# Two-layer hybrid decoder trunk on one Trainium2 core: up products of pairs 2 to 16 joined into 512-column matmuls, the first weight chunk split between two engines, a quarter of the last update on ScalarE and GpSimd

## The chip, the cores and the metric

The kernel runs on one core of one Trainium2 chip. The metric is device time in microseconds (us), lower is better: the median of several executions. The engines are PE (TensorE, the matrix engine, which takes its weights by separate load instructions, PEld), DVE (VectorE), ACT (ScalarE), POOL (GpSimd) and SP (SyncE, which here only issues DMAs). They run side by side and meet at semaphores.

## The reference, cut to what matters

Two layers over 256 positions of 1024 features, fp32. Each layer is an attention half (two attention mixers that are gated and merged) and a gated feed-forward half. The change touches the feed-forward half, the first projection and the last residual update.

```python
def rms_norm(x, gain): ...                    # x * rsqrt(mean(x*x) + EPS) * gain
def conv_ffn(h, w_up, conv_w, conv_b, w_down):
    u = h @ w_up                              # 1024 -> 2 * 2816
    up = jnp.pad(u, ((0, 0), (CONV_WIDTH - 1, 0), (0, 0)))
    c = conv_b
    for k in range(CONV_WIDTH):               # causal, depthwise, width 3
        c = c + conv_w[k] * up[:, k:k + s]
    a, val = jnp.split(c, 2, axis=-1)
    return (jax.nn.gelu(a, approximate=True) * val) @ w_down

def hybrid_layer(x, ...):
    h = rms_norm(x, attn_pre_gain)
    u = h @ w_in                              # the first projection
    ...
    x = x + rms_norm(mixed @ w_out, attn_post_gain)
    h = rms_norm(x, ffn_pre_gain)
    return x + rms_norm(conv_ffn(h, ...), ffn_post_gain)
```

## The kernel before, in words

**Numbers.** Every operand of a matmul is split into a high and a low part (type fp32r): the high part is a rounded copy, the low part what is left. A product is then three matmuls into one PSUM bank: high by high, high by low, low by high. So a tile of weights that arrives as `st` becomes `wh` (a copy on ACT, L114) and `wl` (a subtraction on DVE, L117). These two helper lines carry most of the work of ACT and DVE.

**The weight stream.** The object `W` brings all weights in order: a DMA on SP's queue (L160) into `st` (4 buffers), then the copy and the subtraction into `wh` and `wl` (4 buffers each). A buffer of `wh` is free when PE has used the tile four places earlier in the stream, so ACT's copies follow PE. Some tiles are made ahead of their place into buffers that are idle by then ("early" tiles, with the names kB, sg, kA/vbd and q): in the first layer one at each of the pairs 14 to 17 of the feed-forward loop, in the second only at 14 and 16.

**The feed-forward half** (`ffn_layer`). The 5632 columns of the up projection are 22 pairs j = 0 to 21 of a gate half and a value half, 128 columns each. Pairs 0 and 1 come from `up_first` with another tiling. For j = 2 to 20 a loop runs, in this order on PE:

- `up(j, half)`, twice: for each of 8 blocks k of the features three matmuls 128x256 (L1065 to L1067), moving the tile hh (high), hl (low) and hh again, 24 in all; both halves lie in one bank, T or mm in turn;
- `down(j-2)`: 12 matmuls 128x512 (L388 to L390 in the helper `mm3`) into four banks (named S and O) that gather the result over all j.

`act_gate(j)` stands between them on the other engines: per half a scaled copy of the bank with bias (ACT, L1048) and two multiply-adds shifted by one and two positions (DVE, L1051 and L1052; together the convolution), then the gelu (ACT, L1072), the product of the halves (DVE, L1073), and its split into gh (ACT, L114) and gl (DVE, L117). These small tiles, all named k, come from one pool of 11 buffers.

**The order.** A scheduler sets each engine's order of instructions from the program; on an engine everything runs in that order.

**The start.** The input x is transposed on PE (L432), multiplied by the first gain on DVE (L434) and split by ACT (L114) and DVE (L117) into the tiles named x. The first weight chunk has 2 blocks of 512 columns and is split as a whole (ACT, 128x1024, then DVE). The first 12 products (L457, each 128x512) use it for both halves t of the positions; next on PE are the transposes of the second chunk of x.

**The end.** `post_norm(t)` adds the normed result to X: ACT takes squares (L407), DVE multiplies by the gain (L408), POOL makes the reciprocal root (L376, L377), and DVE does two updates of 128x512 (L413), each followed by its output DMA (L1169).

Of the kernel before, what the change touches and what calls it, by code (L numbers as in the profile page):

```python
# [16 lines left out]
P = 128  # L17
T = 256
# [35 lines left out]
WARM = (6, 2, 3)  # L54
FIRST = [(0, 0), (1, 0), (0, 1), (1, 1), (0, 2), (1, 2), (0, 3), (1, 3)]
# [10 lines left out]
def tile_hybrid_trunk(  # L66
# [78 lines left out]
    class Stream:  # L145
# [31 lines left out]
        def high(self, i):  # L177
# [20 lines left out]
            copy(hi, st)  # L198

            def low():  # L200
                sub(lo, st, r32(hi))
# [12 lines left out]
    TAGS = {"kB": 1, "sg": 2, "q8": 3}  # L214
# [228 lines left out]
    def attn_layer(l, xp, rs, gains, first, order, last_T):  # L443
# [6 lines left out]
        def products(t, c, bk, chs, w):  # L450
            todo = [(tt, p, k) for p in ((0, 0), (0, 1), (1, 0)) for tt in range(2) for k in range(2)] if c == 0 else \
                   [(t, p, k) for p in ((0, 0), (1, 0), (0, 1)) for k in range(2)]
            if c == 0:
                todo = todo[6 * t:6 * t + 6]
# [108 lines left out]
        qA, qB, qR = big8("q8", 3), big8("q8", 3), big8("q8", 3)  # L563
# [148 lines left out]
        def out_T(br, g):  # L712
            if OT[br] is None:
                OT[br] = big8("q8", 3)
# [247 lines left out]
        return yp  # L962

    def out_layer(l, yp, gains, order):
# [34 lines left out]
        hp = big8("q8", 3), big8("q8", 3)  # L999
# [28 lines left out]
        return hp, [lambda: t4_of(xg[1], hp, 1, 0), lambda: (t4_of(xg[1], hp, 1, 1), low())]  # L1028


    def ffn_layer(l, hp, gains, last, order, last_T):
        hh, hl = hp
# [12 lines left out]
        def conv(b, jj, half, then=None):  # L1045
            c = k1()
            u = b[:, half * T:(half + 1) * T]
# [7 lines left out]
        up_bank, up_w, gs, wdn = {}, {}, {}, {}  # L1055

# [12 lines left out]
        def act_gate(j):  # L1069
            b = up_bank.pop(j)  # L1070
            ca, cv = conv(b, j, 0), conv(b, 22 + j, 1)
# [76 lines left out]
        ca = conv(up_bank.pop(j), j, 0)  # L1148
# [4 lines left out]
        cv = conv(up_bank.pop(j), 22 + j, 1, None if last else lambda: lows.append(W.high(nxt[2])))  # L1153
# [57 lines left out]
    def start():  # L1211
# [13 lines left out]
        lw0 = W.high(0)  # L1225
        low0 = first_split(0, 0, m0, xp)
        warm(WARM[1])
        low1 = first_split(1, 0, first_T(1, 0), xp)
        warm(WARM[2])
        lw0()  # L1230
        low0()
# [26 lines left out]
    for l in range(DEPTH):  # L1258

        yp = attn_layer(l, xp, rs, gains, l == 0, order, last_T)  # L1260
        hp, last_T = out_layer(l, yp, gains, order)
# [80 lines left out]
```

## Time and profile before

| what | us |
|---|---|
| device time, median of 3 (lowest, highest) | 775.21 (775.03, 776.46) |
| device time of the profiled execution | 774.85 |
| its span | 772.8 |
| PE busy | 756.8 (98%) |
| DVE busy | 611.1 (79%) |
| ACT busy | 497.9 (64%) |

The profile is of one execution. Its span runs from the first to the last recorded work; 2.05 us of the device time lie around it. A matmul's recorded duration holds the passage through the array, so matmuls that follow each other overlap in the records: what one costs is the distance from its start to the start of the next, and that is read from the timeline.

### The profile page before, as it was taken

To read this page: it belongs to the slowest core of one execution; us is meant where nothing else is said; L and a number is where in the kernel's file an instruction comes from. 1 tells how busy PE (TensorE), PEld (TensorE's weight loads), DVE (VectorE), ACT (ScalarE), POOL (GpSimd) and SP (SyncE) were. 2 spreads that over 40 slices of the span, in tenths; PEclk is the share of its full clock that TensorE was granted. 3 is DMA by queue.
4 is the path that set the end of the run, shared out by engine and by line. 5 is a ranking of instruction groups with operands and counts; after the bars stand their busy time and mean duration, and the time that the engine had idled before them with its cause. 6 is when DMAs were issued, how large, how long until landed. Compare 5 with 4: busy or idle time off the path is not lost.

```text
span 772.8 us, 12863 instructions
## 1 busy us (share of the span) xinstructions
PE 756.8 (98%) x4742; PEld 677.0 (88%) x4742; DVE 611.1 (79%) x1181; ACT 497.9 (64%) x951; POOL 26.9 (3%) x52
## 2 busy tenths in 40 slices
PE   8999999999999999999999999999999999999995
PEld 6888898888899999999878889988888999999994
DVE  7998898687687777777787989985967877777774
ACT  6686986755665555665566979776565655566552
POOL 3000001000000000000010000010010000000000
PEclk9999999999999999999999999999999999999998
DMA  8633265355655556766335224644655656566621
GB/s 333 198 107 122 63 205 190 137 179 178 195 202 182 187 189 191 230 221 209 132 131 157 89 79 136 210 149 148 206 189 163 185 184 191 185 192 219 196 82 55
DMA packets 42345, 131.25 MB, mean 170 GB/s; under 512 B 5375, under 2 KB 5931, under 8 KB 42283
## 3 DMA queue, kind: packets, MB, share of 16 engines
q1 hardware_dynamic: 41707, 129.39, 51.6%
q10 hardware_dynamic: 576, 1.05, 0.4%
q8 instruction: 37, 0.61, 0.3%
q14 instruction: 25, 0.20, 0.1%
HBM read 129.37 MB, written 1.05 MB: 169 GB/s over the span
## 4 chain that ended last, share of the span: by engine, by line
PE 86%; ACT 8%; DVE 3%; issue 1%; DMA 1%; POOL 0%; SPq 0%; DVEq 0%; POOLq 0%; ACTq 0%
PE mm L388 6%; PE mm L389 6%; PE mm L390 6%; PE S L388 5%; PE S L390 5%; PE S L389 5%; PE mm L1067 5%; PE mm L1066 5%; PE mm L1065 5%; PE T L1066 5%; PE T L1065 5%; PE T L1067 5%; PE O L389 4%; PE O L388 4%; PE O L390 4%; ACT k L649 2%
## 5 line engine op out<-in xcount | busy, mean ns | idle before, releaser
L117 DVE TENSOR_TENSOR wl<-st,wh 128x1024 fp32r<-128x1024 f32 (+2 forms) x214 | 253.2, 1184 | 89.4 <-ACT wh L114 86.8
L114 ACT ACTIVATE wh<-st 128x1024 fp32r<-128x1024 f32 (+2 forms) x214 | 219.1, 1027 | 158.1 <-PE mm L1066 36.8
L1065 PE MATMUL mm<-q,wh 128*128 128x256 f32 x336 | 95.1, 283 | 0.0
L1067 PE MATMUL mm<-q,wl 128*128 128x256 f32 x336 | 95.0, 283 | 0.0
L1066 PE MATMUL mm<-q,wh 128*128 128x256 f32 x336 | 95.0, 283 | 0.0
L388 PE MATMUL mm<-wh,x 128*128 128x512 f32 (+2 forms) x240 | 89.8, 374 | 0.1
L389 PE MATMUL mm<-wl,x 128*128 128x512 f32 (+2 forms) x240 | 88.2, 368 | 0.0
L390 PE MATMUL mm<-wh,x 128*128 128x512 f32 (+2 forms) x240 | 88.0, 367 | 0.0
L1066 PE MATMUL T<-q,wh 128*128 128x256 f32 x304 | 86.0, 283 | 0.0
L1067 PE MATMUL T<-q,wl 128*128 128x256 f32 x304 | 86.0, 283 | 0.0
L1065 PE MATMUL T<-q,wh 128*128 128x256 f32 x304 | 85.9, 283 | 0.0
L1065 PEld LDWEIGHTS mm<-q,wh 128*128 128x128 f32 x336 | 64.4, 192 | 0.9
L1066 PEld LDWEIGHTS mm<-q,wh 128*128 128x128 f32 x336 | 64.4, 192 | 0.8
L1067 PEld LDWEIGHTS mm<-q,wl 128*128 128x128 f32 x336 | 64.4, 192 | 0.1
L1065 PEld LDWEIGHTS T<-q,wh 128*128 128x128 f32 x304 | 58.3, 192 | 0.8
L1066 PEld LDWEIGHTS T<-q,wh 128*128 128x128 f32 x304 | 58.3, 192 | 0.7
L1067 PEld LDWEIGHTS T<-q,wl 128*128 128x128 f32 x304 | 58.3, 192 | 0.0
L390 PEld LDWEIGHTS mm<-wh,x 128*128 128x128 f32 x240 | 45.1, 188 | 5.7 <-DVE x L117 0.4
L388 PEld LDWEIGHTS mm<-wh,x 128*128 128x128 f32 x240 | 45.2, 188 | 4.8 <-ACT k L114 0.4
L389 PEld LDWEIGHTS mm<-wl,x 128*128 128x128 f32 x240 | 45.2, 188 | 4.5
L649 ACT ACTIVATE k<-k,mn 128x128 f32<-128x128 f32 (+1 forms) x96 | 42.4, 445 | 7.1 <-DVE mn L646 7.0
L114 ACT ACTIVATE k<-k 128x256 fp32r<-128x256 f32 x72 | 29.1, 413 | 13.0 <-DVE k L1073 6.1
(336 smaller groups left out, 1665.4 us busy)
## 6 DMA issues: line engine op xcount, KB each, us to landing
st<-in_ffn_w_up_dram SPq DMA_DIRECT2D x88, 512.0 KB, 4.0
st<-in_ffn_w_down_dram SPq DMA_DIRECT2D x44, 512.0 KB, 3.6
st<-in_w_in_dram SPq DMA_DIRECT2D x42, 512.0 KB, 3.8
st<-in_w_out_dram SPq DMA_DIRECT2D x16, 512.0 KB, 3.6
st<-in_w_in_dram SPq DMA_DIRECT2D x16, 384.0 KB, 3.2
st<-in_cmp_w_dram SPq DMA_DIRECT2D x16, 256.0 KB, 2.7
st<-in_w_branch_a_dram SPq DMA_DIRECT2D x8, 512.0 KB, 3.5
st<-in_w_branch_b_dram SPq DMA_DIRECT2D x8, 512.0 KB, 3.5
```

What stands on the lines that cost most here:

```text
L114: return act.activation(dst, src, AF.Copy, scale=scale)
L117: return dve.tensor_tensor(dst, a, b, ALU.subtract)
L388: pe.matmul(o, xh, wh, start=first, stop=False, skip_group_check=True)
L389: pe.matmul(o, xh, wl, start=False, stop=False, skip_group_check=True)
L390: pe.matmul(o, xl, wh, start=False, stop=last, skip_group_check=True)
L649: last_exp[0] = act.activation(self.pt[:, hh, s, :], sm[:, :nk], AF.Exp, bias=self.mn[:, i:i + 1], scale=-1.0, accum_out=self.dn[:, i:i + 1])
L1065: pe.matmul(o, wh[:, k, :], hh[:, k, c0:c1], start=(k == 0), stop=False, skip_group_check=True)
L1066: pe.matmul(o, wh[:, k, :], hl[:, k, c0:c1], start=False, stop=False, skip_group_check=True)
L1067: pe.matmul(o, wl[:, k, :], hh[:, k, c0:c1], start=False, stop=(k == 7), skip_group_check=True)
```

## The change

Three edits, one in each of three places.

1. **Pairs 2 to 16 (JOINT).** The high and low parts of the normed input lie side by side in one tile H. `up_joint` runs per block k one matmul of `wh` that moves both parts (512 columns: high by high in the first half of a bank, high by low in the second) and one of `wl` (256 columns, onto the first half). Each half of a pair has a whole bank. `left` then brings the two halves of the bank together: ACT copies the second half to SBUF, DVE adds the first. The convolution reads that sum from SBUF. The three tiles of tag q8 that held these parts and others become H and one q8 tile. Pairs 17 to 21 stay as they were.
2. **The start.** The copy of the first weight chunk is split in two: block 0 on ACT, block 1 on DVE; the copy of x for t = 0 goes ahead of it on ACT; the subtraction too is in two halves; the 12 products come in another order, with those that need x's low part ahead of some that need `wl`.
3. **The last update (t = 1).** Its last 256 of 1024 columns are scaled on ACT and added to X on POOL; DVE does one update of 512 and one of 256 columns. `post_norm` is used here alone.

```diff
+JOINT = range(2, 17)
...
-        def high(self, i):
+        def high(self, i, halves_by=()):
...
-            copy(hi, st)
+            if halves_by:
+                for k, f in enumerate(halves_by):
+                    f(lambda e, k=k: (copy if e is act else dve.tensor_copy)(hi[:, k], st[:, k]))
+            else:
+                copy(hi, st)
...
+                if halves_by:
+                    for k in range(a):
+                        sub(lo[:, k], st[:, k], r32(hi[:, k]))
+                else:
+                    sub(lo, st, r32(hi))
...
     def post_norm(t, banks, gain, follow):
         g, r = norm_a(banks, gain)
+        if t == 1:
+            z = k1()
+            xs = X[:, t, 3 * T:4 * T]
+            act.activation(z, g[1][:, T:2 * T], AF.Identity, bias=0.0, scale=r)
+            pool.tensor_tensor(xs, z, xs, ALU.add)
         for n in range(2):
-            norm_b(t, n, g, r)
+            if t == 1 and n == 1:
+                xs = X[:, t, 2 * T:3 * T]
+                dve.scalar_tensor_tensor(xs, g[1][:, 0:T], r, xs, ALU.mult, ALU.add)
+            else:
+                norm_b(t, n, g, r)
             follow(n)
...
+                todo = [todo[i] for i in (0, 1, 2, 3, 4, 5, 8, 10, 9, 11, 6, 7)][6 * t:6 * t + 6]
...
-        qA, qB, qR = big8("q8", 3), big8("q8", 3), big8("q8", 3)
+        H = ap_.tile([P, 2, KD, T], F32R, tag="h16", name=nm("H"))
+        qA, qB, qR = H[:, 0], H[:, 1], big8("q8", 1)
...
-        def conv(b, jj, half, then=None):
+        def conv(u, jj, then=None):
             c = k1()
-            u = b[:, half * T:(half + 1) * T]
...
+        def up_joint(j, half):
+            b = up_bank[j, half] = bank("mm" if j % 2 == 0 else "T")
+            wh, wl, _ = W.next(8, P)
+            both = b.rearrange("p (s t) -> p s t", s=2)
+            for k in range(8):
+                pe.matmul(both, wh[:, k, :], H[:, :, k, :], start=(k == 0), stop=False, skip_group_check=True)
+                pe.matmul(b[:, 0:T], wl[:, k, :], hh[:, k, :], start=False, stop=(k == 7), skip_group_check=True)
+
+        def left(j, half):
+            if j not in JOINT:
+                return up_bank[j][:, half * T:(half + 1) * T]
+            b = up_bank.pop((j, half))
+            u = k1()
+            copy(u, b[:, T:2 * T])
+            dve.tensor_tensor(u, b[:, 0:T], u, ALU.add)
+            return u
...
-            ca, cv = conv(b, j, 0), conv(b, 22 + j, 1)
+            ua, uv = left(j, 0), left(j, 1)
+            ca, cv = conv(ua, j), conv(uv, 22 + j)
...
-                part(lambda: up(j, half, 0, T))
+                part(lambda: up_joint(j, half) if j in JOINT else up(j, half, 0, T))
...
-        lw0 = W.high(0)
         low0 = first_split(0, 0, m0, xp)
+        by = []
+        lw0 = W.high(0, [by.append, by.append])
+        by[0](act)
...
+        by[1](dve)
         warm(WARM[2])
+        low0()
         lw0()
-        low0()
         low1()
```

**How the order moves.** Numbers behind a name tell one tile from another. First PE, in one half of a pair of the loop, before:

```order
L1065 MATMUL mm_2648<-q_585_2293,wh_2584 128x256
L1066 MATMUL mm_2648<-q_586_2294,wh_2584 128x256
L1067 MATMUL mm_2648<-q_585_2293,wl_2585 128x256
L1065 MATMUL mm_2648<-q_585_2293,wh_2584 128x256
L1066 MATMUL mm_2648<-q_586_2294,wh_2584 128x256
L1067 MATMUL mm_2648<-q_585_2293,wl_2585 128x256
```

and after, the same two blocks of a half and the end of the `down` ahead of them:

```order
L399 MATMUL O_2629<-wh_2639,k_635_2539 128x512
L1084 MATMUL mm_2720<-H_127,wh_2662 128x512
L1085 MATMUL mm_2720<-H_127,wl_2663 128x256
L1084 MATMUL mm_2720<-H_127,wh_2662 128x512
L1085 MATMUL mm_2720<-H_127,wl_2663 128x256
```

Three matmuls of 256 columns have become one of 512 and one of 256, and the two sizes alternate.

Second ACT, through one pair. Before (wh_2930, wh_2960 and wh_3004 are the copies of weights for tiles that PE takes later; T_2834 is the pair's bank):

```order
L114 ACTIVATE wh_2930<-st_2928 128x1024
L1048 ACTIVATE k_697_2895<-T_2834,vec 128x256
L114 ACTIVATE wh_2960<-st_2958 128x1024
L1048 ACTIVATE k_698_2899<-T_2834,vec 128x256
L1072 ACTIVATE k_697_2895<-k_697_2895 128x256
L114 ACTIVATE wh_3004<-st_3002 128x1024
L114 ACTIVATE k_699_2905<-k_697_2895 128x256
```

After (the pair's banks are mm_2720 and mm_2743; the three buffers of weights that follow come free when PE has ended `up(j+1, 0)`, `up(j+1, 1)` and `down(j-1)`):

```order
L115 ACTIVATE wh_2872<-st_2870 128x1024
L115 ACTIVATE k_685_2766<-mm_2720 128x256
L115 ACTIVATE k_686_2769<-mm_2743 128x256
L115 ACTIVATE wh_2891<-st_2889 128x1024
L1069 ACTIVATE k_687_2772<-k_685_2766,vec 128x256
L1069 ACTIVATE k_688_2776<-k_686_2769,vec 128x256
L115 ACTIVATE wh_2914<-st_2912 128x1024
L1111 ACTIVATE k_687_2772<-k_687_2772 128x256
L115 ACTIVATE k_689_2782<-k_687_2772 128x256
```

Two copies out of PSUM are new, and the pair's steps now stand behind other weight copies: before, the first convolution step stood behind the copy into the buffer that the pair's own `up(j, 1)` has just left free; now it stands behind the copy that waits for `up(j+1, 1)`.

DVE in the same place, before:

```order
L117 TENSOR_TENSOR wl_2931<-st_2928,wh_2930 128x1024
L1051 SCALAR_TENSOR_TENSOR k_697_2895<-T_2834,vec,k_697_2895 128x255
L1052 SCALAR_TENSOR_TENSOR k_697_2895<-T_2834,vec,k_697_2895 128x254
L117 TENSOR_TENSOR wl_2961<-st_2958,wh_2960 128x1024
L1051 SCALAR_TENSOR_TENSOR k_698_2899<-T_2834,vec,k_698_2899 128x255
L1052 SCALAR_TENSOR_TENSOR k_698_2899<-T_2834,vec,k_698_2899 128x254
L1073 TENSOR_TENSOR k_697_2895<-k_697_2895,k_698_2899 128x256
L117 TENSOR_TENSOR wl_3005<-st_3002,wh_3004 128x1024
L117 TENSOR_TENSOR k_700_2906<-k_697_2895,k_699_2905 128x256
```

and after:

```order
L118 TENSOR_TENSOR wl_2873<-st_2870,wh_2872 128x1024
L1093 TENSOR_TENSOR k_685_2766<-mm_2720,k_685_2766 128x256
L1093 TENSOR_TENSOR k_686_2769<-mm_2743,k_686_2769 128x256
L118 TENSOR_TENSOR wl_2892<-st_2889,wh_2891 128x1024
L1072 SCALAR_TENSOR_TENSOR k_687_2772<-k_685_2766,vec,k_687_2772 128x255
L1072 SCALAR_TENSOR_TENSOR k_688_2776<-k_686_2769,vec,k_688_2776 128x255
L1073 SCALAR_TENSOR_TENSOR k_687_2772<-k_685_2766,vec,k_687_2772 128x254
L1073 SCALAR_TENSOR_TENSOR k_688_2776<-k_686_2769,vec,k_688_2776 128x254
L118 TENSOR_TENSOR wl_2915<-st_2912,wh_2914 128x1024
L1112 TENSOR_TENSOR k_687_2772<-k_687_2772,k_688_2776 128x256
L118 TENSOR_TENSOR k_690_2783<-k_687_2772,k_689_2782 128x256
```

Two additions are new, and the product and gl now stand one right behind the other.

Third DVE at the start, before (wl_156 is the first weight chunk's low part, the two results L434 are the scaled x of both t):

```order
L434 TENSOR_TENSOR k_68_153<-T_148,gfirst_120 128x512
L434 TENSOR_TENSOR k_72_166<-T_161,gfirst_120 128x512
L117 TENSOR_TENSOR wl_156<-st_83,wh_155 128x1024
L117 TENSOR_TENSOR x_12_119<-k_68_153,x_11_118 128x4x128
L117 TENSOR_TENSOR x_12_119<-k_72_166,x_11_118 128x4x128
```

and after:

```order
L453 TENSOR_TENSOR k_67_152<-T_147,gfirst_120 128x512
L453 TENSOR_TENSOR k_71_165<-T_160,gfirst_120 128x512
L201 CAST wh_155<-st_83 128x512
L118 TENSOR_TENSOR x_12_119<-k_67_152,x_11_118 128x4x128
L118 TENSOR_TENSOR wl_156<-st_83,wh_155 128x512 x2
L118 TENSOR_TENSOR x_12_119<-k_71_165,x_11_118 128x4x128
```

The cast is new on DVE, and the low part of x for t = 0 now stands ahead of that of the weights.

## Rows read from the trace of the kernel before

**Rows 1.** The page's first part (busy time, share of the span and instructions of each engine) and the first line of the chain of waits that ended last, by engine.

```profile
PE 756.8 (98%) x4742; PEld 677.0 (88%) x4742; DVE 611.1 (79%) x1181; ACT 497.9 (64%) x951; POOL 26.9 (3%) x52
...
PE 86%; ACT 8%; DVE 3%; issue 1%; DMA 1%; POOL 0%; SPq 0%; DVEq 0%; POOLq 0%; ACTq 0%
```

**Rows 2.** Busy time by windows of the span. Columns: window, its length, then busy us and instructions of PE, PEld, DVE, ACT and POOL, the granted PE clock, DMA share and GB/s. The first two lie inside the feed-forward loops of the two layers, the third near the start.

```profile
220.00:360.00 140.00, 140.00 (x989) 131.59 (x989) 108.34 (x160) 84.75 (x123) 0.00 (x0) 1.00 0.63 201
...
590.00:750.00 160.00, 160.00 (x1135) 150.55 (x1134) 121.08 (x179) 93.63 (x139) 0.00 (x0) 1.00 0.59 186
...
20.00:30.00 10.00, 10.00 (x47) 8.00 (x46) 10.00 (x16) 6.67 (x9) 0.00 (x0) 1.00 0.88 295
```

**Rows 3.** Timeline of PE where the `up` of one pair ends and its `down` begins (241.04), and the start of the next `down`. Columns: start, duration, engine, line, operation.

```profile
240.80 0.28 PE L1066 MATMUL T<-q,wh 128*128 128x256 f32 x1
240.92 0.28 PE L1067 MATMUL T<-q,wl 128*128 128x256 f32 x1
241.04 0.39 PE L388 MATMUL S<-wh,k 128*128 128x512 f32 x1
241.27 0.39 PE L389 MATMUL S<-wl,k 128*128 128x512 f32 x1
...
243.58 0.39 PE L390 MATMUL O<-wh,k 128*128 128x512 f32 x1
...
249.56 0.39 PE L388 MATMUL S<-wh,k 128*128 128x512 f32 x1
```

**Rows 4.** Timeline of PE in two other places: the first and last of 24 matmuls of 512 columns without a gap, and a change from 512 to 256 columns.

```profile
14.56 0.39 PE L388 MATMUL mm<-wh,x 128*128 128x512 f32 x1
...
19.78 0.39 PE L390 MATMUL mm<-wh,x 128*128 128x512 f32 x1
...
118.98 0.39 PE L390 MATMUL mm<-wh,x 128*128 128x512 f32 x1
119.20 0.28 PE L708 MATMUL O<-k,VT 128*128 128x256 f32 x1
```

**Rows 5.** Groups of instructions by line and shape in 215 to 372 us (the loop of the first layer). Columns: line, engine, operation, out<-in, shapes, count, then busy us and mean ns of one, then idle time before them and what ended it.

```profile
L117 DVE TENSOR_TENSOR wl<-st,wh 128x1024 fp32r<-128x1024 f32 x55 | 67.3, 1223 | 26.9 <-ACT wh L114 25.9
L1052 DVE SCALAR_TENSOR_TENSOR k<-mm,vec,k 128x254 f32<-128x254 f32 x20 | 9.6, 481 | 0.6
L1073 DVE TENSOR_TENSOR k<-k,k 128x256 f32<-128x256 f32 x20 | 8.5, 426 | 2.1
...
L114 ACT ACTIVATE wh<-st 128x1024 fp32r<-128x1024 f32 x55 | 58.2, 1058 | 49.0 <-PE mm L1066 18.1 <-PE O L390 16.0 <-PE T L1066 14.7
L1048 ACT ACTIVATE k<-mm,vec 128x256 f32<-128x256 f32 x20 | 11.0, 550 | 1.4 <-DVE k L1052 1.3
L114 ACT ACTIVATE k<-k 128x256 fp32r<-128x256 f32 x20 | 8.3, 415 | 2.6 <-DVE k L1073 2.6
```

**Rows 6.** Timeline of DVE where the tile gl (L117, 128x256) of one pair is made: first for the pair whose `up` ends at 241.04 [rows 3], then for the tenth pair after it, which has an early tile beside it.

```profile
249.00 0.42 DVE L117 TENSOR_TENSOR k<-k,k 128x256 fp32r<-128x256 f32 x1
...
336.58 0.42 DVE L117 TENSOR_TENSOR k<-k,k 128x256 fp32r<-128x256 f32 x1
```

**Rows 7.** What ACT waited for in 325 to 352 us and in 705 to 732 us (the early tiles of the first and the second layer): us in total, times, longest.

```profile
ACT sg L114 <- DMA st<-in_ffn_w_down_dram: 2.4, 1, 2.4
...
ACT kA L114 <- DMA st<-in_w_in_dram: 1.5, 1, 1.5
...
ACT sg L114 <- DMA st<-in_ffn_w_down_dram: 1.9, 1, 1.9
```

**Rows 8.** Timeline of the start: the scaled x, the first weight copy, the split of x, the first products and the first transposes after the 12 products.

```profile
5.68 0.69 DVE L434 TENSOR_TENSOR k<-T,gfirst 128x512 f32<-128x512 f32 x1 [0.88 <-PE T L432]
...
6.34 1.06 ACT L114 ACTIVATE wh<-st 128x1024 fp32r<-128x1024 f32 x1 [2.23 <-DMA st<-in_w_in_dram]
...
6.73 0.69 DVE L434 TENSOR_TENSOR k<-T,gfirst 128x512 f32<-128x512 f32 x1 [0.36 <-PE T L432]
7.30 1.13 ACT L114 ACTIVATE x<-k 128x512 fp32r<-128x512 f32 x2
7.43 1.23 DVE L117 TENSOR_TENSOR wl<-st,wh 128x1024 fp32r<-128x1024 f32 x1
...
7.97 1.25 PE L457 MATMUL mm<-wh,x 128*128 128x512 f32 x4 [0.59 <-ACT x L114]
...
8.57 1.29 DVE L117 TENSOR_TENSOR x<-k,x 128x512 fp32r<-128x512 f32 x2
...
10.91 1.03 PE L432 MATMUL T<-cst,X 128*128 128x128 f32 x8
```

**Rows 9.** Timeline of the end, from the reciprocal root to the two output DMAs.

```profile
766.22 0.56 POOL L377 TENSOR_TENSOR rstd<-rstd,neg_half 128x1 f32<-128x1 f32 x1
766.81 1.41 DVE L413 SCALAR_TENSOR_TENSOR X<-k,rstd,X 128x512 f32<-128x512 f32 x2 [0.35 <-POOL rstd L377]
767.59 0.99 SPq L1169 DMA_DIRECT2D out_dram<-X  x2
```

**Rows 10.** The two groups of 128x512 operations of POOL with two inputs in SBUF, over the whole span (columns as in rows 5).

```profile
L829 POOL TENSOR_TENSOR vbd<-vq,cst 128x512 fp32r<-128x512 f32 x2 | 3.0, 1523 | 132.6 <-ACT vq L114 132.6
...
L830 POOL TENSOR_TENSOR vbd<-vr,cst 128x512 fp32r<-128x512 f32 x2 | 2.1, 1040 | 0.0
```

More of the change, by code (lines that the diff above doesn't have):

```diff
@@ L212, in next @@
             return self.made[self.used - 1]
-    TAGS = {"kB": 1, "sg": 2, "q8": 3}
+    TAGS = {"kB": 1, "sg": 2, "q8": 1}
     W = Stream()
@@ L450, in products @@
         def products(t, c, bk, chs, w):
-            todo = [(tt, p, k) for p in ((0, 0), (0, 1), (1, 0)) for tt in range(2) for k in range(2)] if c == 0 else \
+            todo = [(tt, p, k) for p in ((0, 0), (1, 0), (0, 1)) for tt in range(2) for k in range(2)] if c == 0 else \
                    [(t, p, k) for p in ((0, 0), (1, 0), (0, 1)) for k in range(2)]
             if c == 0:
-                todo = todo[6 * t:6 * t + 6]
+                todo = [todo[i] for i in (0, 1, 2, 3, 4, 5, 8, 10, 9, 11, 6, 7)][6 * t:6 * t + 6]
             for tt, (xp_, wp_), k in todo:
@@ L713, in out_T @@
             if OT[br] is None:
-                OT[br] = big8("q8", 3)
+                OT[br] = H[:, br]
             bv = OB[br][g].rearrange("p (k c) -> p k c", k=2)
@@ L961, in attn_layer, with out_layer @@
         branch(1)
-        return yp
-    def out_layer(l, yp, gains, order):
+        return yp, H
+    def out_layer(l, yp, H, gains, order):
         gains["ffn_pre"] = gain_tile(ffn_pre_gain, l)
@@ L998, in out_layer @@
             product(0, [k])
-        hp = big8("q8", 3), big8("q8", 3)
+        hp = H[:, 0], H[:, 1]
         g, r = norm_a(res[0], gp)
@@ L1027, in out_layer, with ffn_layer @@
         scaled(1, r)
-        return hp, [lambda: t4_of(xg[1], hp, 1, 0), lambda: (t4_of(xg[1], hp, 1, 1), low())]
-    def ffn_layer(l, hp, gains, last, order, last_T):
-        hh, hl = hp
+        return [lambda: t4_of(xg[1], hp, 1, 0), lambda: (t4_of(xg[1], hp, 1, 1), low())]
+    def ffn_layer(l, H, gains, last, order, last_T):
+        hh, hl = hp = H[:, 0], H[:, 1]
         gains["ffn_post"] = gain_tile(ffn_post_gain, l)
@@ L1147, in ffn_layer @@
         part(lambda: up(j, 0, 0, T))
-        ca = conv(up_bank.pop(j), j, 0)
+        ca = conv(left(j, 0), j)
         act.activation(ca, ca, AF.Gelu_apprx_tanh)
@@ L1152, in ffn_layer @@
         nxt = None if last else [early[l + 1, "in", c] for c in range(4)]
-        cv = conv(up_bank.pop(j), 22 + j, 1, None if last else lambda: lows.append(W.high(nxt[2])))
+        cv = conv(left(j, 1), 22 + j, None if last else lambda: lows.append(W.high(nxt[2])))
         dve.tensor_tensor(ca, ca, cv, ALU.mult)
@@ L1224, in start @@
         m0 = first_T(0, 0)
[L1225 removed]
         low0 = first_split(0, 0, m0, xp)
+        by = []
+        lw0 = W.high(0, [by.append, by.append])
+        by[0](act)
         warm(WARM[1])
[L1228 removed]
+        m1 = first_T(1, 0)
+        low1 = first_split(1, 0, m1, xp)
+        by[1](dve)
         warm(WARM[2])
+        low0()
         lw0()
[L1231 removed]
         low1()
@@ L1258, in tile_hybrid_trunk @@
     for l in range(DEPTH):
-        yp = attn_layer(l, xp, rs, gains, l == 0, order, last_T)
-        hp, last_T = out_layer(l, yp, gains, order)
-        xp, rs, last_T = ffn_layer(l, hp, gains, l == DEPTH - 1, order, last_T)
+        yp, H = attn_layer(l, xp, rs, gains, l == 0, order, last_T)
+        last_T = out_layer(l, yp, H, gains, order)
+        xp, rs, last_T = ffn_layer(l, H, gains, l == DEPTH - 1, order, last_T)
     idle(50)
```

2 lines of the change are left out of this document (removed).

## The prediction

> **What bounds the kernel now.** Read the busy times first, then the chain of waits, then busy times by window, then the timeline of PE. PE is busy for 98% of the span and holds 86% of the chain [rows 1]. In both feed-forward loops it is busy without a break: 140.00 of 140 us and 160.00 of 160 us, at full granted clock, while DVE has 77% and ACT 61% of the first [rows 2]. So there time comes off only if PE's own work gets shorter, and stays off only if ACT and DVE still deliver in time.
>
> What PE's work costs is the distance between starts. In the `up` matmuls of 256 columns it is 0.12 us, in the `down` matmuls of 512 columns (243.58 − 241.04) / 11 = 0.231 us; one pair takes 249.56 − 241.04 = 8.52 us, which is 48 × 0.120 + 12 × 0.231 = 8.53 [rows 3]. Elsewhere 512 columns cost (19.78 − 14.56) / 23 = 0.227 us [rows 4].
>
> **Joint products.** Per block k and half, three matmuls (0.360 us) become one of 512 columns and one of 256. The step from 256 to 512 columns costs 0.12 us [rows 3], that from 512 to 256 columns 0.22 us in the one place shown [rows 4]; I take the two longer rates of 512 columns, 0.227 and 0.231, as bounds for it. The new pair then costs 0.347 to 0.351 us and saves 9 to 13 ns. There are 15 pairs × 2 halves × 8 blocks × 2 layers = 480 such steps: 4.3 to 6.2 us, or 9.6 us if the 0.22 of the single place (read to 0.01 us) held everywhere. I take 12.5 ns, near the 0.227, since most rows outside `down` lie there: **−6.0 us**, a pair taking 8.32 us.
>
> The Trainium skill prices this otherwise: its page "TensorE: Matmul & The Clock Gate", section "Back-to-back issue gap", gives a warm matmul N / 2.4 ns for N columns plus 2.5 ns. By that only the fixed 2.5 ns of one matmul is saved per block, 480 × 2.5 ns = 1.2 us. The rows disagree: 256 columns cost 0.120 us here, where its formula gives 0.109.
>
> **The added work and the slack.** Each pair gets two ACT copies 128x256 out of PSUM and two DVE additions. No row shows these two; nearest are ACT's k copy (0.415 us) below and its PSUM read with bias (0.550) above, and DVE's product (0.426) and multiply-add (0.481) [rows 5]. For DVE a pair is then three weight subtractions of 1.22 us, four multiply-adds of 0.48, and product, gl and two additions of about 0.43: 3.67 + 1.92 + 1.72 = 7.3 us, against 6.45 before. The product and gl now stand one behind the other with ACT's gh copy (0.42) between them, an idle 0.5 us on DVE, so about 7.8 of 8.32 us. ACT does three weight copies of 1.06, two new copies of 0.42, two convolution steps of 0.55, gelu and gh of about 0.41: 5.9 us. Both fit, so I price the additions at nothing in the steady loop; their cover is PE's 8.32 us, with 0.5 us to spare on DVE, and each 0.1 us of a pair beyond it would cost 3 us over 30 pairs.
>
> What shrinks is the lead. Before, gl of the pair whose `up` ends at 241.04 is done at 249.42 [rows 6]; its `down` starts two pairs later, at 249.56 + 8.52 = 258.08: 8.7 us of slack. After, the pair's convolution stands behind the weight copy that waits for `up(j+1, 1)`, and its gelu behind the one that waits for `down(j-1)`. From the end of that `down(j-1)`: the weight copy ends at 1.06 us, its subtraction on DVE at 2.28, the product at 2.7, gh at 3.1 and gl at 3.55. `down(j)` starts behind `up(j+2)`, 16 × 0.347 = 5.55 us after that point, and needs gl for its third matmul, 0.46 later. **Slack 2.4 us** in place of 8.7.
>
> **The early tiles** are what can use it up. Before, ACT waits 2.4 and 1.5 us for DMAs of such tiles in the first layer [rows 7], and gl of the tenth pair after the one above is done at 337.00, where ten periods would put it at 249.42 + 85.2 = 334.6: 2.4 us late [rows 6], covered by 8.7. After, the same lateness stands against 2.4. An early tile also adds 1.22 us to DVE's 7.8 of 8.32, so that each of four pairs in a row may fall back by another 0.7. Bounds: 0 (the DMAs come sooner, or DVE's idle time takes it up) and 4 us (four pairs at 0.7, and 1.2 of a DMA that then comes later); taken **+0.9**, the fall-back of about one pair, since before, the lateness did not grow from pair to pair. In the second layer there are two such tiles, a pair apart, and the one wait is 1.9 us [rows 7], under the slack: nothing.
>
> **The start.** Before, the first product waits until 7.97 for ACT's copy of x, which stands behind the weight copy (6.34 to 7.40); the transposes behind the 12 products start at 10.91 [rows 8]. After, ACT copies x at once (scaled x is there at 6.37), then half the weights; DVE casts the other half behind the second scaling (7.42). No row shows such a cast; half of the 1.23 us subtraction with one input less lies between 0.35 and 0.7. So the first products start near 7.5, but DVE then has x's low part (0.6), two halves of `wl` (1.2) and x's second low part (0.6) to do, ending near 10.3 instead of 9.86, and the last two of the 12 products need that last one. They end at 10.6 to 10.85, and the transposes come 0.05 to 0.3 us sooner. DVE is busy for all of 20 to 30 us [rows 2], and what it does before is only a little more. **−0.1 us**, bounds −0.4 and +0.2.
>
> **The end.** Two DVE updates take 766.81 to 768.22 [rows 9]. After, DVE does 512 and 256 columns, to about 767.95; ACT scales its quarter by about 767.35, and POOL adds it. POOL's 512 columns took 1.04 and 1.52 us [rows 10]; half of that, 0.5 to 0.8, with a full 1.04 as upper end since a part may not scale, ends at 767.9 to 768.4. Taken 768.1: **−0.1 us**, bounds −0.3 and +0.2.
>
> The Trainium skill, page "SBUF — State Buffer", section "Who interferes with whom", speaks against this edit: a DVE instruction with two inputs in SBUF and a GpSimd instruction that reads SBUF exclude each other for their whole length. By it POOL and the second DVE update would run one after the other, to about 768.7, +0.5 instead of −0.1. No row of before has both at once, so it stays outside the sum.
>
> **The sum.** 774.85 − 6.0 + 0.9 − 0.1 − 0.1 = 769.55 on the profiled execution, which lies 0.36 under the median; I say **769.6 us**.
>
> **Rivals.**
>
> *Late gl through the early tiles (0.17).* The stall is 2 to 4 us in the first layer and perhaps 1 in the second: 771 to 774. For it: the lead falls from 8.7 to 2.4 us, and DVE has no room to catch up in those pairs. Against it: behind ACT's waits for DMAs DVE stands idle too, and part of what it has more to do falls there.
>
> *The alternation costs more (0.06).* If the change from 512 to 256 columns costs 0.24 us or moving two separate stretches of H costs some ns more, nothing or little is gained: 480 × 0.360 against 480 × (0.12 + 0.235) leaves 2.4 us, 0.24 leaves none: 773 to 775.5. Against it: the 0.22 in the one row [rows 4].
>
> *Little is saved per matmul (0.03).* A 512-column matmul among 256-column ones costs nearly twice one of these, 0.2375 us where 0.24 is two: 480 × 2.5 ns = 1.2 us less, 774.3 with the other terms. Against it: no row of 512 columns is slower than 0.231. The section "Back-to-back issue gap" named above would give this time.
>
> *Slower: DVE sets the pace of the loop (0.08).* The place is the chain through both engines, copy, addition, convolution, gelu, product, gh, gl, between weight tiles that also need both. I put it at 7.8 us a pair. It decides from 8.53 us: an addition out of PSUM of 0.6 us and another idle wait of 0.5 would do. At 8.9 us the 30 pairs lose 30 × (8.9 − 8.53) = 11 us: 786. For it: DVE is at 77% in the loop already [rows 2]. Against it: most of its idle time there, 25.9 us, is waiting for weight copies, and these wait for PE [rows 5].
>
> *More than forecast (0.04).* 512 to 256 at 0.22 throughout: 480 × 20 ns = 9.6 us, 766.
>
> **How the numbers follow.** The forecast (0.62) spans 767.9 to 772. Chances: forecast 0.62, early tiles 0.17, alternation 0.09, DVE 0.08, more 0.04. A range from 767.8 to 773.8 holds the forecast, nearly all of the early tiles and a little of the others, 0.8. A measurement of this kernel can tell about 0.2% (1.55 us) from no change: faster is below 773.66. The forecast, the larger gain, most of the early tiles and a part of the alternation make 0.84; within 0.2% are the rest of the alternation, the little saving and the end of the early tiles, 0.08; slower is DVE's case, 0.08.
>
> **What would show it.** Starts in the joint part: 0.12 from 256 to 512 columns, 0.227 back, a pair every 8.32 us in both layers. PE in the loops without a break except at pairs 14 to 18 of the first layer, where a wait of `down`'s first matmul for k (gh or gl) of about 1 us would show. gl done 2 us ahead of its need. At the start the first product near 7.5 and the transposes near 10.8; at the end POOL's addition done near 768.1. Wrong would be: waits of PE at every pair (DVE's case), pairs of 8.45 us or more without waits (the alternation), or several us of waits in the pairs 14 to 18.

## The result

The changed kernel takes 771.15 us (median of 4 runs, 769.77 to 771.75), the kernel before 775.12 (774.74 to 776.46): a ratio of 0.9946, 95% interval 0.9931 to 0.9960. A control beside the experiments gave 770.39 against 774.78, 0.9943 (0.9931 to 0.9956). So it is about 4 us faster, inside the range, and 0.8 to 1.6 us above the 769.6 that was forecast.

Single executions of one kernel mostly differ by 1.5 to 2 us, in several kernels in two groups (the joint products alone: 769.44, 769.65, 769.86 and 771.06, 771.13). A place where 1.3 us come from is shown with experiment e3. The profiled execution of the changed kernel took 771.28 us with a span of 768.3: 3.0 us lie around the span, where it is 1.8 in its other executions. The sum of parts at the end therefore goes by the profiles of the two controls, of 774.83 and 770.39 us.

### The profile page after: what moved, and what is told of

It is laid out like the page before. It is cut to its first block, busy times and chain, and to the rows that moved or that the text cites. A ratio compares the mean times of both kernels' runs of the same rounds, so it can differ in the third digit from the quotient of the medians.

```text
span 768.3 us, 12121 instructions
## 1 busy us (share of the span) xinstructions
PE 753.0 (98%) x4262; PEld 651.3 (85%) x4262; DVE 627.6 (82%) x1243; ACT 513.8 (67%) x1012; POOL 27.6 (4%) x53
## 4 chain that ended last, share of the span: by engine, by line
PE 86%; ACT 8%; DVE 4%; issue 1%; POOL 1%; DMA 0%; DVEq 0%; SPq 0%; ACTq 0%
PE mm L1084 8%; PE T L1084 7%; PE mm L397 6%; PE mm L398 6%; PE mm L399 6%; PE S L397 5%; PE S L399 5%; PE S L398 5%; PE mm L1085 4%; PE O L398 4%; PE O L399 4%; PE O L397 4%; PE T L1085 3%; PE T L698 2%; ACT k L671 2%; ACT k L115 1%
## 5 line engine op out<-in xcount | busy, mean ns | idle before, releaser
L118 DVE TENSOR_TENSOR wl<-st,wh 128x1024 fp32r<-128x1024 f32 (+3 forms) x215 | 253.5, 1180 | 70.5 <-ACT wh L115 66.9
L115 ACT ACTIVATE wh<-st 128x1024 fp32r<-128x1024 f32 (+3 forms) x214 | 218.4, 1024 | 111.3 <-PE O L399 24.3
L1084 PE MATMUL mm<-H,wh 128*128 128x512 f32 x256 | 90.5, 396 | 0.0
L1084 PE MATMUL T<-H,wh 128*128 128x512 f32 x224 | 79.2, 395 | 0.0
L1085 PE MATMUL mm<-H,wl 128*128 128x256 f32 x256 | 71.8, 281 | 0.0
L1085 PE MATMUL T<-H,wl 128*128 128x256 f32 x224 | 62.8, 280 | 0.0
L1084 PEld LDWEIGHTS mm<-H,wh 128*128 128x128 f32 x256 | 48.1, 188 | 11.1
L1084 PEld LDWEIGHTS T<-H,wh 128*128 128x128 f32 x224 | 42.1, 188 | 9.8
L1085 PEld LDWEIGHTS mm<-H,wl 128*128 128x128 f32 x256 | 48.4, 189 | 0.7
L1085 PEld LDWEIGHTS T<-H,wl 128*128 128x128 f32 x224 | 42.3, 189 | 0.7
```

What stands on the lines that cost most here:

```text
L115: return act.activation(dst, src, AF.Copy, scale=scale)
L118: return dve.tensor_tensor(dst, a, b, ALU.subtract)
L1084: pe.matmul(both, wh[:, k, :], H[:, :, k, :], start=(k == 0), stop=False, skip_group_check=True)
L1085: pe.matmul(b[:, 0:T], wl[:, k, :], hh[:, k, :], start=False, stop=(k == 7), skip_group_check=True)
```

## The profile after

The page's busy times and its chain by engine [rows 1]: PE has lost 3.8 us and 480 matmuls, and DVE and ACT have gained 16.5 and 15.9 us.

```profile
PE 753.0 (98%) x4262; PEld 651.3 (85%) x4262; DVE 627.6 (82%) x1243; ACT 513.8 (67%) x1012; POOL 27.6 (4%) x53
...
PE 86%; ACT 8%; DVE 4%; issue 1%; POOL 1%; DMA 0%; DVEq 0%; SPq 0%; ACTq 0%
```

The two loops by window [rows 2]: PE is still busy without a break, the early tiles of the first layer included, while DVE went from 77 to 84%. The joint pairs do not wait there.

```profile
220.00:360.00 140.00, 140.00 (x782) 121.74 (x781) 117.00 (x191) 93.71 (x156) 0.00 (x0) 1.00 0.62 203
590.00:750.00 160.00, 159.93 (x921) 140.17 (x920) 129.67 (x212) 102.30 (x171) 0.00 (x0) 1.00 0.56 183
```

What a pair costs is in PE's timeline [rows 3, 4], here the first starts of two pairs and of what follows them:

```profile
235.36 0.40 PE L1084 MATMUL T<-H,wh 128*128 128x512 f32 x1
235.59 0.28 PE L1085 MATMUL T<-H,wl 128*128 128x256 f32 x1
235.71 0.39 PE L1084 MATMUL T<-H,wh 128*128 128x512 f32 x1
...
240.91 0.39 PE L397 MATMUL S<-wh,k 128*128 128x512 f32 x1
...
243.69 0.39 PE L1084 MATMUL mm<-H,wh 128*128 128x512 f32 x1
243.91 0.28 PE L1085 MATMUL mm<-H,wl 128*128 128x256 f32 x1
...
244.38 0.40 PE L1084 MATMUL mm<-H,wh 128*128 128x512 f32 x1
244.62 0.28 PE L1085 MATMUL mm<-H,wl 128*128 128x256 f32 x1
244.74 0.40 PE L1084 MATMUL mm<-H,wh 128*128 128x512 f32 x1
...
249.33 0.39 PE L397 MATMUL S<-wh,k 128*128 128x512 f32 x1
...
252.13 0.40 PE L1084 MATMUL T<-H,wh 128*128 128x512 f32 x1
```

The pair in T takes 240.91 − 235.36 = 5.55 us, 0.347 a block, as forecast. The pair in mm takes 5.64 us, 0.3525 a block; its steps of 512 columns are 0.22 to 0.24 apart in place of 0.23. The two kinds alternate through the whole loop. With the `down` behind each (2.78 and 2.80) two pairs take 252.13 − 235.36 = 16.77 us, 8.385 each: 0.14 less than before, where 0.20 was forecast.

DVE's groups in 215 to 336 us and ACT's there, for the added work [rows 5]. ACT's copy out of PSUM takes 0.37 us, less than the 0.42 that was taken, and DVE's addition 0.42, as taken. gl waits for ACT's gh, 4.8 us over 15 pairs:

```profile
L118 DVE TENSOR_TENSOR k<-k,k 128x256 fp32r<-128x256 f32 x15 | 6.3, 423 | 4.8 <-ACT k L115 4.8
...
L1093 DVE TENSOR_TENSOR k<-mm,k 128x256 f32<-128x256 f32 x14 | 5.2, 416 | 0.0
...
L115 ACT ACTIVATE k<-mm 128x256 f32<-128x256 f32 x14 | 4.5, 369 | 0.0
```

gl in DVE's timeline, in the steady loop and ten pairs on with an early tile beside it [rows 6], and ACT's waits for the early tiles of the first layer in 323 to 343 us [rows 7]:

```profile
247.02 0.43 DVE L118 TENSOR_TENSOR k<-k,k 128x256 fp32r<-128x256 f32 x1 [0.48 <-ACT k L115]
...
331.95 0.42 DVE L118 TENSOR_TENSOR k<-k,k 128x256 fp32r<-128x256 f32 x1
```

```profile
ACT kA L115 <- DMA st<-in_w_in_dram: 1.3, 1, 1.3
ACT sg L115 <- DMA st<-in_ffn_w_down_dram: 1.3, 1, 1.3
```

gl is done at 247.45. Its `down` starts at 249.33, and the third matmul of it, the first that reads gl, at 249.79: 2.3 us of lead. Ten pairs of 8.385 later it would be done at 331.3, and is at 332.37: 1.1 us late, within the lead. The same early tiles are waited for 1.3 us each, not 2.4 and 1.5.

The end [rows 9], from DVE's, POOL's and ACT's timeline: DVE's 256 columns take 0.94 us beside POOL's addition, and end 0.28 us behind it.

```profile
763.11 0.51 ACT L430 ACTIVATE k<-k,rstd 128x256 f32<-128x256 f32 x1 [1.07 <-POOL rstd L386]
763.11 0.75 DVE L422 SCALAR_TENSOR_TENSOR X<-k,rstd,X 128x512 f32<-128x512 f32 x1 [0.35 <-POOL rstd L386]
763.69 0.75 POOL L431 TENSOR_TENSOR X<-k,X 128x256 f32<-128x256 f32 x1 [0.62 <-ACT k L430]
763.78 0.94 DVE L435 SCALAR_TENSOR_TENSOR X<-k,rstd,X 128x256 f32<-128x256 f32 x1
```

## The experiments

Every kernel but the controls starts from the changed one or takes parts of it back. "Joint part" below is the time from the first matmul of pair 2 to the first of pair 16 in PE's timeline, 14 of the 15 joint pairs; it is 120.17 and 120.19 us in the two layers before, 118.34 and 118.30 after.

**Controls.** The kernel before and the changed one again.

> The kernel before again, for a second profile. Theory: PE's last matmul ends near 765.0, the last update near 768.2, and the output DMA takes 3.4 to 4.6 us from there, by chance; device time 774.8. Rival: the 4.57 us of the first profile belong to the kernel, and it shows again.

> The changed kernel again, beside the others of this call. Theory: the single executions fall into two groups about 1.3 us apart, according to whether the granted clock falls to 0.66 in 50 to 55 us, behind the 0.78 us gap of PE at 50.2 us, as it did in the profile of the run with the update out of PSUM; without it the kernel is at 769.6, with it at 771.1. By the traces it stands 3.7 us under the kernel before up to PE's last matmul. Rival: it stays at 771.2 in nearly all executions, and the joint products alone (769.86) are better by what start and update cost.

The kernel before: 774.81 us, last update done at 768.29, end of the span at 772.8: the 4.5 us belong to it. The changed kernel: 770.39 (769.62 to 771.00, 5 runs), between the two groups that were expected. Its profile has a granted clock of 1.00 in 50 to 55 us, so a fall of the clock there isn't what holds this execution above 769.6; its first joint matmul starts at 209.42, late with x (see the start, below). Joint parts 118.35 and 118.35. From the first to the second PE's last matmul comes 3.42 us sooner, the last update needs 0.19 more behind it, and the end of the span follows 0.97 sooner on that.

**e1, the joint products alone.** Start and last update of before.

```diff
-            act.activation(z, g[1][:, T:2 * T], AF.Identity, bias=0.0, scale=r)
-            pool.tensor_tensor(xs, z, xs, ALU.add)
...
-                dve.scalar_tensor_tensor(xs, g[1][:, 0:T], r, xs, ALU.mult, ALU.add)
...
-        lw0 = W.high(0, [by.append, by.append])
+        lw0 = W.high(0)
...
-                todo = [todo[i] for i in (0, 1, 2, 3, 4, 5, 8, 10, 9, 11, 6, 7)][6 * t:6 * t + 6]
+                todo = todo[6 * t:6 * t + 6]
```

> Of the three edits only the joint products stay; start and last update are those of before. Theory: the whole of the gain is PE's shorter up products, 3.85 us by the two traces (1.90 in the first layer, 1.95 in the second), so about 771.3 and a ratio of 0.995; the late start of the transposes (11.18 against 10.91) was x arriving 0.37 us later, not the edit, so the transposes of this kernel may start at 10.9 or 11.2 according to x. Rival: the last update brought the 1.0 us that the output DMA took less (4.58 to 3.58 us from the last update's end to the end of the span), then this kernel is at 772.2; or the start lost 0.3 us and the update 0.2, then it is at 770.7.

769.86 us (5 runs), ratio 0.9938 (0.9926 to 0.9951). Joint parts 118.35 in both layers. This is no worse than all three edits together (770.39); but the rival's 772.2 does not come, and the theory's 771.3 neither: the last 1.2 us of gain are in the output DMA, without the new update (e7).

**e2, no joint pair.**

```diff
-JOINT = range(2, 17)
+JOINT = range(0)
```

> The start and the last update of the changed kernel and its tile H, but no joint pair. Theory: every pair takes 8.53 us as before, PE waits nowhere in the loops, and the time is that of before within 0.5 us (774.7 to 775.6). Rival as in the run of the joint products alone: 774.1 if the last update brings 1 us, 775.6 if start and update lose 0.5.

773.74 us, ratio 0.9988 (0.9979 to 0.9996), below what theory and rival gave: the joint parts are back at 120.17 and 120.18, and 1.0 us of gain stays. It is again in the output DMA: 3.53 us from the last update to the end, where the kernel before has 4.57.

**e3, the last update out of PSUM.**

```diff
-        g = [k2(), k2()]
+        g = [banks[0], banks[1]] if inplace else [k2(), k2()]
...
-        g, r = norm_a(banks, gain)
+        g, r = norm_a(banks, gain, t == 1)
```

> The changed kernel, but in the last update the product with the gain stays in PSUM, so that DVE's two updates read one operand from SBUF instead of two. In the changed kernel DVE's 256 columns took 0.94 us beside POOL's addition (763.69 to 764.44), with 0.48 for the same form alone. Theory (the two engines shut each other out where both of DVE's inputs lie in SBUF): DVE's 256 columns take about 0.48 us here, POOL's addition its 0.75, and the last update ends about 0.3 us sooner behind the reciprocal root, with POOL last. Rival (256 columns of this form are slow by themselves, or writing to the same tile X is what holds them): 0.9 us again.

DVE's and POOL's timeline of its end:

```profile
764.58 0.75 DVE L422 SCALAR_TENSOR_TENSOR X<-O,rstd,X 128x512 f32<-128x512 f32 x1 [0.35 <-POOL rstd L386]
765.25 0.47 DVE L435 SCALAR_TENSOR_TENSOR X<-O,rstd,X 128x256 f32<-128x256 f32 x1
...
765.13 0.73 POOL L431 TENSOR_TENSOR X<-k,X 128x256 f32<-128x256 f32 x1 [0.58 <-ACT k L430]
```

0.47 us in place of 0.94, at the same time as POOL's addition into the same tile. So it is the second operand in SBUF that holds DVE. The profile of e5 shows the other order, with both operands of DVE in SBUF: there DVE starts 0.10 us ahead of POOL and takes 0.48, and it is POOL that takes 0.95 instead of 0.75. So 256 columns of this form aren't slow by themselves; the one that starts second is held.

```profile
767.81 0.48 DVE L435 SCALAR_TENSOR_TENSOR X<-k,rstd,X 128x256 f32<-128x256 f32 x1
767.91 0.95 POOL L431 TENSOR_TENSOR X<-k,X 128x256 f32<-128x256 f32 x1 [1.07 <-ACT k L430]
```

From PE's last matmul the update is done after 3.08 us; before it took 3.21, in the changed kernel 3.41. The time, 770.49 us, doesn't show these 0.3 us, because in this profile, and by their times in two of four runs, something else cost 1.3 us. The windows by which it is seen:

```profile
45.00:50.00 5.00, 4.45 (x35) 3.80 (x34) 4.65 (x21) 4.04 (x15) 0.00 (x0) 1.00 0.34 108
50.00:55.00 5.00, 4.22 (x24) 4.05 (x23) 3.46 (x18) 4.16 (x16) 0.00 (x0) 0.66 0.00 0
```

PE stands still for 0.78 us until 50.95, waiting for ACT, and then the granted clock is 0.66 in 50 to 55 us: matmuls of 280 columns start 0.23 us apart (280 / 1.2 GHz), in the other profiles 0.13 behind the same gap at a granted clock of 1.00.

**e4, two and two.**

```diff
-            for k in range(8):
+            for k2_ in range(0, 8, 2):
+                for k in (k2_, k2_ + 1):
+                    pe.matmul(both, wh[:, k, :], H[:, :, k, :], start=(k == 0), stop=False, skip_group_check=True)
+                for k in (k2_, k2_ + 1):
+                    pe.matmul(b[:, 0:T], wl[:, k, :], hh[:, k, :], start=False, stop=(k == 7), skip_group_check=True)
```

> The joint products of two blocks in the order 512, 512, 256, 256 columns in place of 512, 256, 512, 256. Theory (every matmul costs its columns and a fixed part, wherever it stands): nothing changes, 0.347 to 0.353 us a block, time within 0.7 us of the changed kernel. Rival (the change of size costs): half as many changes; if a change costs the 5 ns by which a block is dearer than 0.1200 + 0.2265, a block falls to 0.345 or less and the time by 1.2 us or more.

769.51 us (4 runs), 0.9 under the control of the changed kernel, where at most 0.7 was expected. In the profiles 0.7 of that comes before the loops: the first joint matmul starts at 208.71, not 209.42, with x there earlier. All pairs take 5.58 us now and all `down` 2.80, in sum 8.38 a pair; joint parts 118.26 and 118.28. Halving the number of changes of size moves nothing of account. The theory stands for the sum; that pairs alternate is gone.

**e5, joint to 20.**

```diff
-JOINT = range(2, 17)
+JOINT = range(2, 21)
```

> Pairs 2 to 20 joint in place of 2 to 16. Theory (PE sets the pace, 0.144 us saved per pair): 8 pairs more save 1.1 us, less the stalls where the early tiles now meet joint pairs only and the last pairs follow without a down between: at best 768.6, PE without waits up to pair 18. Rival (the lead of gl, 1.9 us, is used up by pairs 17 to 20, where gl has to catch up with an early tile beside it): PE waits of 0.5 to 3 us for k at the downs there, time the same as the changed kernel or 1 to 2 us above.

775.71 us, ratio to before 1.0003 (0.9992 to 1.0015): the whole gain is lost. What PE waited for in 330 to 400 us, where the changed kernel has 0.3 us:

```profile
PE mm L1104 <- DVE k L1093: 2.4, 1, 2.4
PE S L397 <- ACT k L115: 0.6, 1, 0.6
...
PE T L1104 <- DVE k L1093: 0.3, 1, 0.3
```

The largest is not gl's: pair 21 waits for its bank, which DVE's late addition still reads. To these 3.3 us comes a last update that ends 4.18 us behind PE's last matmul in place of 3.41, since pair 20 now has the longer way through ACT and DVE. The profiled execution took 774.18 us. The seven executions above 774.5 have a mean granted clock of 0.993 to 0.995, the three from 773.96 to 774.18 have 0.998; where the clock falls in the longer ones no profile shows.

**e6, two more DVE instructions.**

```diff
             dve.tensor_tensor(ca, ca, cv, ALU.mult)
+            if j in JOINT:
+                for _ in range(2):
+                    dve.scalar_tensor_tensor(ca, ca, 0.0, ca, ALU.mult, ALU.add)
```

> The changed kernel with two more DVE instructions of 128x256 (0.48 us each, times 0 plus itself) behind the product of every joint pair: about 0.9 us more of DVE's work per pair, and of the way from copy to gl. Theory (DVE's loop is at 7.8 to 7.9 of 8.38 us): the loop becomes 8.7 us, PE waits at every joint pair once the lead is used up, 30 pairs x 0.3 us less the lead of two layers (2 x 1.0 us) = 5 to 9 us more, 776 to 780. Rival (DVE's idle time is free for the taking, 7.3 of 8.38 busy): DVE gets to 8.2 of 8.38, and only the lead shrinks: the time stays within 1 us.

781.72 us, 11.3 more than the changed kernel, yet by neither theory. To pair 17 the first layer takes 7.2 us longer and the second 4.0. In the steady pairs of both layers PE doesn't wait (240 to 290 and 620 to 670 us: 50.00 of 50): the two added instructions of 0.43 us find room. The waits are at the early tiles; here for the first layer, in 300 to 345 us:

```profile
PE S L397 <- ACT k L115: 3.8, 3, 1.8
PE mm L1084 <- DVE k L1093: 1.3, 1, 1.3
```

The second layer has 3.0 us. The rest is in matmuls that start farther apart behind such waits: in 340.1 to 342.2 us of the first layer those of 512 columns are 0.40 to 0.43 apart, about 512 / 1.2 GHz, at a granted clock of 0.50. Besides the added work the order differs from that of the changed kernel: the scheduler puts a weight subtraction between the added instructions and gl.

**e7, the tile alone.** The kernel before with H in place of two of the three q8 tiles; as a diff to the kernel before:

```diff
-        qA, qB, qR = big8("q8", 3), big8("q8", 3), big8("q8", 3)
+        H = ap_.tile([P, 2, KD, T], F32R, tag="h16", name=nm("H"))
+        qA, qB, qR = H[:, 0], H[:, 1], big8("q8", 1)
...
-        hp = big8("q8", 3), big8("q8", 3)
+        hp = H[:, 0], H[:, 1]
```

> The kernel before with only the tile H in place of the tiles q8: no joint pair, start and last update as before. Theory: the output DMA, which takes 4.5 us from the last update to the end of the span in both profiles of before and 3.4 to 3.6 us in all six kernels with H, follows where the tiles lie in memory, so this kernel has the 3.4 to 3.6 us too and the time is 773.7. Rival: the 4.5 us come back here, 774.8; then joint pairs and the new start or update each shorten it in another way.

773.98 us against 774.78, a ratio of 0.9992 (0.9983 to 1.0001), so the medians alone don't show a gain. Six of ten runs lie between 773.41 and 774.06, 0.7 to 1.4 under before, at a mean granted clock of 0.998 or 0.999; the other four lie between 775.13 and 775.27, at 0.996 or 0.997. In the profile (773.90 us) the last update is done at 768.44 and the span ends at 771.8: 3.36 us, as the theory said.

That the tiles' place in memory does it is not shown, and the traces hold another reason. The DMA queues in 768.2 to 772 us, first of the control before, then of e7 (packets, MB, share of 16 engines; in the last row KB and us to landing):

```profile
q1 hardware_dynamic: 288, 0.52, 37.3%
q14 instruction: 1, 0.01, 0.5%
out_dram<-X SPq DMA_DIRECT2D x1, 256.0 KB, 3.1
```

```profile
q1 hardware_dynamic: 288, 0.52, 36.9%
out_dram<-X SPq DMA_DIRECT2D x1, 256.0 KB, 2.0
```

In both profiles of before, one packet of 8 KB of the queue of kind "instruction" falls into the last output DMA: it starts at 770.12 (770.10 in the control) and takes 0.31 us. The last packet of the output DMA comes only behind it, at 770.43 (770.50), 0.5 us after the last of the 31 other 4-byte packets, and the landing 1.0 us after that. In e7 the nearest instruction packet is at 767.41, ahead of that DMA; its last packet comes with the others, and the landing 0.36 us later. In none of the twelve profiles with H does an instruction packet fall between issue and landing of the last output DMA. No run moves this packet alone, so that it costs the 1.0 us is read from these times, not tried.

So about 1 us of the change's gain comes with the edit of the tile, in the output DMA, and has nothing to do with what the edits are for.

**e8, mirrored.**

```diff
+                def big():
+                    pe.matmul(both, wh[:, k, :], H[:, :, k, :], start=(k == 0), stop=(k == 7), skip_group_check=True)
+                def little():
+                    pe.matmul(b[:, 0:T], wl[:, k, :], hh[:, k, :], start=False, stop=False, skip_group_check=True)
+                for f in ((big, little) if k % 2 == 0 else (little, big)):
+                    f()
```

> The changed kernel with each second block of a joint half the other way about: 512, 256, 256, 512 columns. If a matmul costs its columns and a fixed part, a pair and its down take 8.38 us as in both orders so far. If what makes every other pair 0.09 us dearer (5.644 against 5.551 us) hangs on the strict turn of the two sizes, both kinds of pairs fall to 5.58 as with two and two, or to 5.55.

A single execution: 768.72 us. All pairs take 5.57 us with 2.80 for the `down`, 8.37; joint parts 118.02 and 117.99, 0.3 us a layer less than in the changed kernel. So the pairs alternate only where the sizes turn strictly; both other orders end it.

**e9 and e10, both improvements.** Two and two, or mirrored, with the update out of PSUM (edits as in e3, e4 and e8).

> Joint products in the order 512, 512, 256, 256, and the last update with its product in PSUM. Theory: the two add, 0.05 us from the order and 0.33 from the update; 769.3 where the clock does not fall in 50 to 55 us, the fastest of these kernels by a margin that is too small to be told from the two-and-two kernel (769.5). Rival: no sum, 769.5 to 770.4.

> The mirrored order of the joint products (512, 256, 256, 512) and the last update with its product in PSUM. Theory: the joint part of a layer is 118.0 us as in the mirrored look (118.34 in the changed kernel), the last update 0.33 us shorter: 768.7 or a little less in most executions, about 1.5 more where the clock falls in 50 to 55 us; under the changed kernel (770.39) and the kernel before (774.78). Rival: the 768.72 of one look was chance in start and end, and the median is 769.4 as with two and two.

e9: 769.38 us (5 runs), as expected no sure gain over e4. e10: 768.74 (768.46 to 770.50, 5 runs) against 774.89, ratio 0.9925 (0.9911 to 0.9938); joint parts 118.00 and 118.05, the update 3.07 us behind PE's last matmul. It is the fastest kernel of the case, 1.6 us under the control of the changed one. Between the two profiles about half of the difference lies before the loops (first joint matmul at 208.46 against 209.42, x there 1.25 us earlier), which neither edit touches; whether that comes again isn't shown. The loops bring 0.7 and the update 0.3.

## Why the prediction was right, and where not

What the gain rests on was forecast: PE sets the pace of both loops and its work got shorter. That the number fell into the range is in part luck, because errors cancel: the joint products brought 2.0 us less than forecast and the update lost 0.2 instead of bringing 0.1, while a stall of 0.9 did not come and 1.0 us was gained where nothing was forecast. (The sum of 769.55 also stood on the profiled execution; on the median, 0.36 above it, it would have been 769.9.)

**Joint products: the mechanism right, the size too large.** Forecast −6.0 us. From the first matmul of pair 2 to the first of pair 17 the layers take 126.79 and 126.63 us after, 128.69 and 128.72 before: −4.0, a little under the lower bound of 4.3. Half of the pairs cost the 0.347 a block that was taken, the other half 0.3525, and the `down` behind those 0.02 more. The rows of before did not show it, for no place there alternates the two sizes for long. That makes 0.14 us a pair, 4.3 us for 30 pairs. The remaining 0.3 us are lost at pairs 2 and 3: in the first layer from 208.91 to 226.76 us before and 209.17 to 226.92 after, 0.10 saved in place of 0.29. The weight load of the first `down` waits 0.3 us for k there; how much of the loss that is wasn't followed.

**Lead and early tiles: right in kind, +0.9 too much.** The lead of gl, counted to the third matmul of its `down`, was put at 2.4 us and is 2.3. What was too much is its lateness at an early tile, taken from before (2.4): it is 1.1, with DMA waits of 1.3 in place of 2.4 us. So nothing is lost. e6 shows that the place was the right one: it is there, and not in the steady loop, that more work on DVE stops PE.

**DVE's pace: too dark.** It was put at 7.8 of 8.32 us with idle time counted in, and to decide from 8.53. e6 adds 0.85 us of work and the steady pairs still don't wait: the idle time that was counted (DVE waiting for gh) is filled there by a weight subtraction, which the scheduler has put ahead of gl.

**Start: between −0.2 and +0.25, by when x comes.** Forecast −0.1, bounds −0.4 and +0.2. What bounds the new start is the second scaled x: the transposes come 4.07, 4.06, 4.06 and 4.06 us behind the start of that scaling in the profiles of the changed kernel, its control, e2 and e3. With the old start they came at 10.91, 10.92, 11.17 and 11.11 us (before, control, e1, e7), with scalings at 6.73, 6.21, 7.36 and 7.26. So at equal x the new start gains 0.15 us with the scaling at 6.70 (10.76 in e2) and 0.6 at 6.22 (10.28 in e4), and loses 0.25 at 7.36 (11.42 in the control). At the first matmul of pair 2 gains of 0.2 and 0.2 and a loss of 0.25 are left of this (208.72 against 208.91 before, 208.71 against 208.93 in its control, 209.42 against 209.17 in e1). DVE's cast took 0.42 us.

**Last update: wrong by 0.3 us.** Forecast −0.1, measured +0.2 (3.21 to 3.41 us behind PE's last matmul). The step that failed is that DVE's 256 columns take about 0.45 beside POOL: they take 0.94. The rule that was weighed, from the Trainium skill's "SBUF — State Buffer", "Who interferes with whom", is borne out by e3, 0.94 against 0.47, and by the turned order in e5; the loss that the prediction worked out by it was 0.5 where 0.2 came, since DVE ended 0.28 us behind POOL and not a whole 0.47.

**What was not in the sum: −1.0 us in the output DMA**, which comes with the tile H (e7); in both profiles of before an instruction packet falls into that DMA, in none with H. Between the profiles of the two controls the sum closes: the first matmul of pair 2 0.49 us later (half of it x, half the new start where x is late), joint pairs −3.92, update +0.19, output −0.97, around the span −0.24, together −4.45; their device times are 774.83 and 770.39. Without the output's part the change would have brought 3.5 us, and the forecast, −5.25, would have been 1.8 too good.

The rival that the Trainium skill's page "TensorE: Matmul & The Clock Gate", section "Back-to-back issue gap", would give (2.5 ns per block, 1.2 us) falls: a block saves 0.360 − 0.350 = 10 ns.

## What to carry to other kernels

On a bound engine, price a change of the pattern from starts in that pattern, and where no row has it, from the worse of the neighbouring rates. When work is moved to engines with spare time, ask where their lead is smallest, not whether their mean share fits: here there was room in every steady pair, and none at four early tiles. Before an update is shared between VectorE and GpSimd, see where VectorE's operands lie: here the shared update lost 0.2 us with both in SBUF and gained 0.1 with one in PSUM (3.41 and 3.08 against 3.21).

## What the runs showed of the hardware

- Matmuls of 512 and 256 columns in strict turn settle into one of two rhythms per pair, 5.55 and 5.64 us, that follow each other; which comes first differs between the layers and between profiles of the same loop (in the first layer the banks mm have 5.64 in the changed kernel and 5.55 in e3). So it isn't the bank alone. Mirrored blocks settle into one rhythm of 5.57, two and two into 5.58. What beats there stays open.
- VectorE's update of 256 columns with both operands in SBUF and GpSimd's addition hold each other up, whichever starts second: VectorE takes 0.94 us where GpSimd starts first (changed kernel), GpSimd 0.95 where VectorE does (e5), against 0.47 and 0.73 with one operand of VectorE in PSUM (e3).
- The end of the span came 4.5 us behind the last update in both profiles of before and 3.4 to 3.7 in every kernel with H. In the first two, and in no other, an 8 KB instruction packet of 0.31 us falls into the last output DMA, whose last packet and landing come late; the times name it as the cause, no run tried it alone. Why the packet comes at another time with H was not followed.
- The granted clock fell to a mean of 0.66 in 50 to 55 us behind a gap of PE of 0.78 us in the profile of e3, with matmuls at the lower level, 1.2 GHz, while the same gap in the others left it at 1.00. It costs 1.3 us. Where executions fall into two clear groups, the longer ones have a lower mean granted clock (e7: 0.996 or 0.997 against 0.998 or 0.999).
